# One-hot gate tiles laid out in pairs of tokens, with columns 4 bytes apart in place of 8

## The chip, the core and the metric

The kernel runs on one core of a Trainium2 chip. The metric is device time in microseconds of one execution; lower is better. The engines named below are TensorE (PE in the profile, its weight loads PEld), VectorE (DVE), ScalarE (ACT), GpSimd (POOL), and the DMA queues, which SyncE issues (SP).

## What is computed

One decoder layer for 256 tokens of width 1024: a combined input projection, a convolution module and a sparse attention, an output projection, a memory cross-attention, and at the end a mixer of experts (`peer`) with a final RMSNorm. The change lies in the expert mixer. Each token n picks 8 x 16 = 128 experts out of 16384; an expert's number is a pair (i1, i2) of numbers below 128, and each pick has a gate:

```
def chunk(args):
    xc, ec, gc = args
    u = u_emb[ec]
    a = jax.nn.gelu(jnp.einsum('nd,nkd->nk', xc, u))
    return jnp.einsum('nk,nkd->nd', gc * a, v_emb[ec])
```

The kernel does not gather rows of `u_emb` and `v_emb`. It computes the activations of all 16384 experts for all tokens, multiplies them by a gate that is zero where an expert was not picked, and multiplies the product by all of `v_emb`.

## The kernel before

**Stages.** All activations lie transposed, with features on the 128 partitions and the 256 tokens along the free dimension. Projections in fp32 run as three matmuls in fp32r, on a high and a low part of each operand: `wchunk` (lines 143 to 145) loads 128x1024 weights into a `raw` tile, ScalarE rounds each half to `hi` (line 137), and VectorE (in some stages GpSimd) subtracts to get `lo` (line 138). `proj` and `mm3` (lines 147 to 154) then run 8 x 3 matmuls of 256 columns for a chunk. The tags `hi` and `lo` have six buffers of half a chunk each, `raw` has four.

The expert mixer has three stages.

1. Lines 994 to 999: the first J = 36 chunks of u (128 experts each), whose gelu goes to `slA`. In the last turns the picks of each token are transposed: `i1T`, `i2T` and `gTh`, `gTl` (the gate's high and low fp16 part) are [128 picks, 256 tokens] in fp16.
2. Lines 1024 to 1038, the fused stage: the other 92 chunks of u, and between them 64 turns of `gates4`, one for each four tokens. The loop runs a turn as soon as `ng` falls behind `(i - J) * T // (KEYS - 3 - J)`, so there are 64 turns over 89 chunks.
3. Lines 1073 to 1096: the 128 chunks of v, multiplied by the gated activations and summed in the four PSUM tiles Y.

**A turn of gates4** (lines 1004 to 1022). For four tokens it builds four one-hot tiles on VectorE with 512 fp16 elements per partition. A partition is a pick; the elements are 128 values i times 4 tokens j. `o1` is 1 where i equals the pick's i1 (line 1011), `o2` the same for i2 (line 1012), `oh` and `ol` are `o2` times the high and the low part of the gate (lines 1013, 1014). TensorE multiplies, for each token j, `o1[:, :, j]` (the weights, which are loaded anew for each of the two matmuls) by `oh[:, :, j]` and then by `ol[:, :, j]` (the moving operand; lines 1016, 1017) and sums the two in the PSUM tile `pw`: the 128x128 matrix of this token's gates by (i1, i2). The profile writes the four one-hot tiles all as `o`. VectorE multiplies `pw` into the activations that are there already (line 1021), and ScalarE copies the rest into `slB` (line 1022), for later chunks to be multiplied into (line 1034).

In the old layout the four tokens of one value i lie side by side, so from one value i to the next within one token's tile there are 4 elements, or 8 bytes. The lines that say it:

```
o1, o2, oh, ol = [tmp.tile([P, P, 4], F16, ...) for t in range(4)]
V.tensor_tensor(o1, iota4, over_i(i1T), op=ALU.is_equal)
PE.matmul(pw[:, j], o1[:, :, j], oh[:, :, j], start=True, stop=False)
PE.matmul(pw[:, j], o1[:, :, j], ol[:, :, j], start=False, stop=True)
```

**Order of the work.** TensorE's instructions run in the order in which they are written (`manual_schedule`, line 97); the scheduler orders those of the other engines. `o1`, `oh` and `ol` have two buffers each, `o2` one; `pw` has two PSUM banks (tag `w`), the `pu` tiles of the chunks two others (tag `s`).

One row used below lies elsewhere: line 482 (`ph`) multiplies weights by every 16th f32 column of a tile `KV`, so that its moving columns lie 64 bytes apart. Lines 560 and 883 are matmuls on dense bf16 tiles, lines 442, 591, 596 and 843 on plain f32.

Of the kernel before, what the change touches and what calls it, by code (L numbers as in the profile page):

```python
# [12 lines left out]
F16 = mybir.dt.float16  # L13
# [3 lines left out]
ALU = mybir.AluOpType  # L17
# [3 lines left out]
P = 128  # L21
# [71 lines left out]
def build(tc, A, out, dbg=None):  # L93
    nc = tc.nc
    V, S, G, PE = nc.vector, nc.scalar, nc.gpsimd, nc.tensor
# [13 lines left out]
    def C(name):  # L109
        a, b = CC[name]  # L110
        return con1[:, a:b] if b <= NCON1 else con2[:, a - NCON1:b - NCON1]
# [50 lines left out]
    i1T, i2T, gTh, gTl = [tk.tile([P, T], F16, name=n) for n in ("i1T", "i2T", "gTh", "gTl")]  # L162
# [314 lines left out]
    for i in range(2):  # L477
# [3 lines left out]
        for jj in range(16):  # L481
            PE.matmul(phv, w1[i][:, jj], KV[i][:, :, 2 * jj:2 * jj + 16 * (NC_CMP - 1) + 1:16],
                      start=(jj == 0), stop=(jj == 15))
# [398 lines left out]
    for nh, c in ((0, 0), (1, 0), (1, 1), (0, 1)):  # L882
        PE.matmul(Y[nh][c], zero[:, 0:P], zero, start=True, stop=False, skip_group_check=True)
        for k in range(4):
            PE.matmul(Y[nh][c][:, k * P:(k + 1) * P], h2T[:, 4 * c + k, nh * P:(nh + 1) * P], C("ident"),
                      start=False, stop=False, skip_group_check=True)
# [9 lines left out]
    for hf in range(2):  # L896
# [36 lines left out]
        for side in range(2):  # L933
# [12 lines left out]
            oh = tp.tile([P, 16, P], F16, name=f"ohx{hf}{side}", tag="ohx")  # L946
# [36 lines left out]
    e1 = outer.enter_context(tc.tile_pool(name="e1", bufs=1, side="left", **RW))  # L983
    slA = e1.tile([P, J, T], F32, name="slA")
    tmp = outer.enter_context(tc.tile_pool(name="tmp", bufs=2, side="left", **RW))
    iota4 = tmp.tile([P, P, 4], F16, name="iota4", bufs=1)
    V.tensor_copy(iota4, C("iota").unsqueeze(2).to_broadcast([P, P, 4]))

    def u_chunk(i):
        ps = pp.tile([P, 512], F32, name=f"pu{i}", tag="w" if i < J - 8 and i % 4 > 1 else "s", bufs=2)[:, 0:T]  # L990
# [12 lines left out]

    def gates4(n0, done):
        pw = pp.tile([P, 512], F32, name=f"pw{n0}", tag="w", bufs=2).rearrange("p (n i) -> p n i", n=4)
        o1, o2, oh, ol = [tmp.tile([P, P, 4], F16, name=f"o{t}{n0}", tag=f"o{t}", bufs=1 if t == 1 else 2) for t in range(4)]

        def over_i(t):
            return t[:, n0:n0 + 4].unsqueeze(1).to_broadcast([P, P, 4])

        V.tensor_tensor(o1, iota4, over_i(i1T), op=ALU.is_equal)
        V.tensor_tensor(o2, iota4, over_i(i2T), op=ALU.is_equal)
        V.tensor_tensor(oh, o2, over_i(gTh), op=ALU.mult)  # L1013
        V.tensor_tensor(ol, o2, over_i(gTl), op=ALU.mult)
        for j in range(4):
            PE.matmul(pw[:, j], o1[:, :, j], oh[:, :, j], start=True, stop=False)  # L1016
            PE.matmul(pw[:, j], o1[:, :, j], ol[:, :, j], start=False, stop=True)  # L1017
        for sl_, x0, x1 in ((slA, 0, J), (slB, J, done)):
            if x1 > x0:
                va = sl_[:, 0:x1 - x0, n0:n0 + 4].rearrange("p i n -> p n i")  # L1020
                V.scalar_tensor_tensor(va, pw[:, :, x0:x1], 1.0 / GSC, va, op0=ALU.mult, op1=ALU.mult)  # L1021
        S.activation(slB[:, done - J:, n0:n0 + 4].rearrange("p i n -> p n i"), pw[:, :, done:], AF.Copy, scale=1.0 / GSC)  # L1022

    i, ng = J, 0
    while i < KEYS or ng < T:
        if i < KEYS:
            ps = u_chunk(i)
            if ng:
                tt = tmp.tile([P, T], F32, name=f"ua{i}", tag="ua", bufs=3)
                S.activation(tt[:, 0:ng], ps[:, 0:ng], AF.Gelu_apprx_tanh)  # L1030
            if ng < T:
                S.activation(slB[:, i - J, ng:], ps[:, ng:], AF.Gelu_apprx_tanh)
            if ng:
                V.tensor_mul(slB[:, i - J, 0:ng], slB[:, i - J, 0:ng], tt[:, 0:ng])
            i += 1
        while ng < min(T, (i - J) * T // (KEYS - 3 - J)):
            gates4(ng, i)
            ng += 4
# [35 lines left out]
    for i in range(KEYS):  # L1074
        a = slA[:, i] if i < J else slB[:, i - J]
# [94 lines left out]
```

## Time and profile before

| | |
|---|---|
| median of 3 runs | 1144.11 us (1143.82 to 1146.87) |
| the profiled execution, its own time | 1143.92 us |
| its span in the trace | 1142.1 us |
| TensorE busy | 1095.2 us, 96% |
| TensorE weight loads busy | 1005.4 us, 88% |
| VectorE busy | 884.2 us, 77% |
| ScalarE busy | 591.8 us, 52% |
| GpSimd busy | 111.2 us, 10% |
| mean granted clock of TensorE | 0.984 of full speed |

The span is the time from the first to the last record of the trace; the time of the execution is 1.8 us longer. Busy time counts stretches in which at least one record of the engine is open. A TensorE record includes the passage through the array, so successive records overlap, and the cost of a matmul in a full stream is the distance from its start to the next start, not its length. The records of VectorE overlap a little as well.

### The profile page before, as it was taken

To read this page: it belongs to the slowest core of one execution; us is meant where nothing else is said; L and a number is where in the kernel's file an instruction comes from. 1 tells how busy PE (TensorE), PEld (TensorE's weight loads), DVE (VectorE), ACT (ScalarE), POOL (GpSimd) and SP (SyncE) were. 2 spreads that over 40 slices of the span, in tenths; PEclk is the share of its full clock that TensorE was granted. 3 is DMA by queue.
4 is the path that set the end of the run, shared out by engine and by line. 5 is a ranking of instruction groups with operands and counts; after the bars stand their busy time and mean duration, and the time that the engine had idled before them with its cause. 6 is when DMAs were issued, how large, how long until landed. Compare 5 with 4: busy or idle time off the path is not lost.

```text
span 1142.1 us, 20622 instructions
## 1 busy us (share of the span) xinstructions
PE 1095.2 (96%) x7361; PEld 1005.4 (88%) x7362; DVE 884.2 (77%) x2229; ACT 591.8 (52%) x1354; POOL 111.2 (10%) x86
## 2 busy tenths in 40 slices
PE   8889999999999489999999999999999999999997
PEld 7878778999999489999999999999888888888885
DVE  7998847888889994778888889996666666666665
ACT  5731456665455155555555554445555555555554
POOL 0000000000068389000000000000000000000000
PEclk9899999999999889999999999999999999999999
DMA  8542224625434235544444454446555566565662
GB/s 277 194 127 94 74 99 152 197 90 185 154 124 149 93 114 200 167 156 141 150 147 160 137 161 137 151 144 203 191 196 193 194 192 195 192 196 191 196 192 86
DMA packets 51688, 182.47 MB, mean 160 GB/s; under 512 B 5761, under 2 KB 6529, under 8 KB 51457
## 3 DMA queue, kind: packets, MB, share of 16 engines
q1 hardware_dynamic: 51296, 180.62, 48.2%
q8 instruction: 58, 0.95, 0.3%
q10 hardware_dynamic: 288, 0.52, 0.1%
q14 instruction: 46, 0.37, 0.1%
HBM read 179.81 MB, written 1.05 MB: 158 GB/s over the span
## 4 chain that ended last, share of the span: by engine, by line
PE 87%; DVE 4%; issue 3%; POOL 2%; DMA 1%; ACT 1%; SPq 0%; POOLq 0%; ACTq 0%; DVEq 0%
PE Y L1070 30%; PE pu L150 10%; PE pu L149 10%; PE pu L148 10%; PE pw L1016 3%; PE pw L1017 3%; PE pmk L442 3%; POOL lo L138 2%; PE pmv L458 2%; PE ppq L148 1%; PE ppq L149 1%; PE ppq L150 1%; DVE lo L138 1%; PE pmw L149 1%; PE pmw L148 1%
## 5 line engine op out<-in xcount | busy, mean ns | idle before, releaser
L137 ACT ACTIVATE hi<-raw 128x512 fp32r<-128x512 f32 x632 | 380.6, 624 | 198.7 <-PE pu L149 78.0
L138 DVE TENSOR_TENSOR lo<-raw,hi 128x512 fp32r<-128x512 f32 (+1 forms) x560 | 371.1, 685 | 32.8 <-ACT hi L137 26.4
L148 PE MATMUL pu<-hn_h,hi 128*128 128x256 f32 x1024 | 296.9, 290 | 18.3 <-ACT hi L137 18.3
L150 PE MATMUL pu<-hn_h,lo 128*128 128x256 f32 x1024 | 291.6, 285 | 2.5 <-POOL lo L138 2.5
L149 PE MATMUL pu<-hn_l,hi 128*128 128x256 f32 x1024 | 290.8, 284 | 0.0
L148 PEld LDWEIGHTS pu<-hn_h,hi 128*128 128x128 f32 x1024 | 198.0, 193 | 18.7 <-ACT hi L137 18.5
L150 PEld LDWEIGHTS pu<-hn_h,lo 128*128 128x128 f32 x1024 | 196.7, 192 | 4.6 <-POOL lo L138 4.5
L149 PEld LDWEIGHTS pu<-hn_l,hi 128*128 128x128 f32 x1024 | 197.2, 193 | 0.0
L1070 PE MATMUL Y<-hi,ah 128*128 128x512 f32 x512 | 158.2, 389 | 0.0
L1070 PE MATMUL Y<-lo,ah 128*128 128x512 f32 x512 | 158.1, 389 | 0.0
L1070 PE MATMUL Y<-hi,al 128*128 128x512 f32 x512 | 158.1, 389 | 0.0
L1070 PEld LDWEIGHTS Y<-lo,ah 128*128 128x128 f32 x512 | 96.1, 188 | 20.0
L1070 PEld LDWEIGHTS Y<-hi,al 128*128 128x128 f32 x512 | 96.1, 188 | 19.8
L1070 PEld LDWEIGHTS Y<-hi,ah 128*128 128x128 f32 x512 | 96.1, 188 | 19.9
L158 DVE TENSOR_TENSOR al<-slB,ah 128x256 fp32r<-128x256 f32 x92 | 39.1, 425 | 89.9 <-PE Y L1070 89.9
L138 POOL TENSOR_TENSOR lo<-raw,hi 128x512 fp32r<-128x512 f32 x72 | 103.7, 1473 | 36.6 <-ACT hi L137 36.3
L157 ACT ACTIVATE ah<-slB 128x256 fp32r<-128x256 f32 x92 | 38.5, 418 | 115.7 <-PE Y L1070 115.7
L1022 ACT ACTIVATE slB<-pw 128x364 f32<-128x364 f32 (+31 forms) x64 | 33.3, 521 | 67.3 <-DVE slB L1021 50.1
L1017 PE MATMUL pw<-o,o 128*128 128x128 f16 x256 | 64.2, 297 | 0.0
L1016 PE MATMUL pw<-o,o 128*128 128x128 f16 x256 | 63.6, 294 | 0.0
L273 DVE SCALAR_TENSOR_TENSOR yc<-u,par,yc 128x256 f32<-128x256 f32 x120 | 55.9, 477 | 0.3
L1013 DVE TENSOR_TENSOR o<-o,gTh 128x512 f16<-128x512 f16 x64 | 28.5, 445 | 30.9 <-PE pw L1016 30.5
(387 smaller groups left out, 1754.1 us busy)
## 6 DMA issues: line engine op xcount, KB each, us to landing
raw<-u SPq DMA_DIRECT2D x128, 512.0 KB, 3.3
raw<-v SPq DMA_DIRECT2D x128, 512.0 KB, 4.3
raw<-peer_w_q SPq DMA_DIRECT2D x16, 512.0 KB, 3.3
raw<-w_in_t SPq DMA_DIRECT2D x15, 512.0 KB, 6.0
raw<-w_mem_k SPq DMA_DIRECT2D x8, 512.0 KB, 3.4
raw<-w_mem_v SPq DMA_DIRECT2D x8, 512.0 KB, 3.4
raw<-w_out SPq DMA_DIRECT2D x8, 512.0 KB, 3.9
raw<-w_mem_q SPq DMA_DIRECT2D x8, 512.0 KB, 3.3
```

The costliest lines, as they stand in the source:

```text
L137: S.activation(hi, r, AF.Copy)
L138: (engs or (V, V))[q].tensor_sub(lo, r, hi.bitcast(F32))
L148: PE.matmul(ps, w[0], xh, start=start, stop=False)
L149: PE.matmul(ps, w[0], xl, start=False, stop=False)
L150: PE.matmul(ps, w[1], xh, start=False, stop=stop)
L157: S.activation(dst[0], src, AF.Copy)
L158: V.tensor_sub(dst[1], src, dst[0].bitcast(F32))
L273: V.scalar_tensor_tensor(yc[:, i], u[:, i, j:j + T], w, yc[:, i], op0=ALU.mult, op1=ALU.add)
L442: PE.matmul(ps, wr[:, k * P:(k + 1) * P], mg[:, k], start=(k == 0), stop=(k == KC - 1))
L1016: PE.matmul(pw[:, j], o1[:, :, j], oh[:, :, j], start=True, stop=False)
L1017: PE.matmul(pw[:, j], o1[:, :, j], ol[:, :, j], start=False, stop=True)
L1070: PE.matmul(Y[nh][c], lhs[:, sl], wc[c][t], start=False, stop=i == KEYS - 1 and lhs is a[1], skip_group_check=True)
```

## The change

The one-hot tiles become [128, 2, 128, 2]: two blocks of two tokens. Within a block the two tokens of one value i lie side by side, so that within one token's tile the step from one value i to the next is 2 elements, or 4 bytes. The tile with the numbers 0 to 127 is repeated twice in place of four times and read by both blocks. Nothing else is changed: the number of instructions, their order on each engine, the sizes of the matmuls and of the four VectorE operations, the buffers and the values are the same. The only instruction with another count of elements is the copy that fills the tile of numbers (line 987), which has 256 elements per partition in place of 512. The lines behind line 1008 have higher numbers in the changed kernel (the one-hot operations one more, the matmuls and what follows two more).

```diff
-    iota4 = tmp.tile([P, P, 4], F16, name="iota4", bufs=1)
-    V.tensor_copy(iota4, C("iota").unsqueeze(2).to_broadcast([P, P, 4]))
+    iota2 = tmp.tile([P, P, 2], F16, name="iota2", bufs=1)
+    V.tensor_copy(iota2, C("iota").unsqueeze(2).to_broadcast([P, P, 2]))
...
-        o1, o2, oh, ol = [tmp.tile([P, P, 4], F16, name=f"o{t}{n0}", tag=f"o{t}", bufs=1 if t == 1 else 2) for t in range(4)]
+        o1, o2, oh, ol = [tmp.tile([P, 2, P, 2], F16, name=f"o{t}{n0}", tag=f"o{t}", bufs=1 if t == 1 else 2) for t in range(4)]

         def over_i(t):
-            return t[:, n0:n0 + 4].unsqueeze(1).to_broadcast([P, P, 4])
-
-        V.tensor_tensor(o1, iota4, over_i(i1T), op=ALU.is_equal)
-        V.tensor_tensor(o2, iota4, over_i(i2T), op=ALU.is_equal)
+            return t[:, n0:n0 + 4].rearrange("p (a b) -> p a b", b=2).unsqueeze(2).to_broadcast([P, 2, P, 2])
+
+        i4 = iota2.unsqueeze(1).to_broadcast([P, 2, P, 2])
+        V.tensor_tensor(o1, i4, over_i(i1T), op=ALU.is_equal)
+        V.tensor_tensor(o2, i4, over_i(i2T), op=ALU.is_equal)
         V.tensor_tensor(oh, o2, over_i(gTh), op=ALU.mult)
         V.tensor_tensor(ol, o2, over_i(gTl), op=ALU.mult)
         for j in range(4):
-            PE.matmul(pw[:, j], o1[:, :, j], oh[:, :, j], start=True, stop=False)
-            PE.matmul(pw[:, j], o1[:, :, j], ol[:, :, j], start=False, stop=True)
+            q, r = j // 2, j % 2
+            PE.matmul(pw[:, j], o1[:, q, :, r], oh[:, q, :, r], start=True, stop=False)
+            PE.matmul(pw[:, j], o1[:, q, :, r], ol[:, q, :, r], start=False, stop=True)
```

## Rows read from the trace of the kernel before

**Rows 1.** The matmuls into pw: number, shortest, median, longest ns, first and last start.

```profile
L1016 PE MATMUL pw<-o,o x256: 285/296/301, 463.6 to 774.3; 128*128 128x128 f16 x128
L1017 PE MATMUL pw<-o,o x256: 293/297/301, 463.7 to 774.4; 128*128 128x128 f16 x128
```

**Rows 2.** Stretch, length, busy PE, PEld, DVE, ACT, POOL; granted clock, DMA share, GB/s.

```profile
463.00:778.50 315.50, 315.50 (x2640) 312.00 (x2639) 270.69 (x642) 164.47 (x419) 0.00 (x0) 1.00 0.46 149
...
623.00:703.00 80.00, 80.00 (x671) 79.12 (x670) 70.00 (x163) 41.12 (x108) 0.00 (x0) 1.00 0.46 150
703.00:778.50 75.50, 75.50 (x633) 74.68 (x632) 70.30 (x153) 36.68 (x101) 0.00 (x0) 1.00 0.45 150
778.50:1142.10 363.60, 355.92 (x1601) 295.78 (x1599) 227.60 (x413) 192.05 (x395) 2.77 (x1) 0.99 0.57 185
```

**Rows 3.** Timeline of one turn, matmuls and loads together: start us, length us, instruction.

```profile
602.33 0.29 PE L1016 MATMUL pw<-o,o 128*128 128x128 f16 x1
...
602.44 0.12 PEld L1016 LDWEIGHTS <-o 128*128 128x128 f16 x1
602.56 0.30 PE L1016 MATMUL pw<-o,o 128*128 128x128 f16 x1
...
603.15 0.29 PE L1017 MATMUL pw<-o,o 128*128 128x128 f16 x1
...
603.40 0.28 PE L149 MATMUL pu<-hn_l,hi 128*128 128x256 f32 x1
...
603.52 0.28 PE L150 MATMUL pu<-hn_h,lo 128*128 128x256 f32 x1
```

**Rows 4.** Groups of matmuls by shape: number, busy us, mean ns, idle time.

```profile
L149 PE MATMUL pu<-hn_l,hi 128*128 128x256 f32 x1024 | 290.8, 284 | 0.0
L1070 PE MATMUL Y<-hi,ah 128*128 128x512 f32 x512 | 158.2, 389 | 0.0
...
L843 PE MATMUL psq<-skp,pqt 128*128 128x128 f32 x64 | 9.2, 274 | 0.0
...
L482 PE MATMUL ph<-KV,w 128*128 128x45 f32 x64 | 8.9, 272 | 0.0
...
L560 PE MATMUL pss<-causb,identb 128*128 128x128 bf16 x32 | 4.6, 224 | 0.0
...
L883 PE MATMUL Y<-zero 128*128 128x512 bf16 x3 | 1.1, 378 | 0.9 <-ACT sco L846 0.9
```

**Rows 5.** The same view for weight loads.

```profile
L149 PEld LDWEIGHTS pu<-hn_l,hi 128*128 128x128 f32 x1024 | 197.2, 193 | 0.0
...
L1016 PEld LDWEIGHTS <-o 128*128 128x128 f16 x256 | 29.6, 116 | 3.1
...
L596 PEld LDWEIGHTS po<-PT,vn 128*64 128x64 f32 x32 | 3.0, 136 | 1.3 <-issue 1.3
...
L560 PEld LDWEIGHTS <-identb 128*128 128x128 bf16 x32 | 1.8, 97 | 4.0 <-issue 2.9
...
L591 PEld LDWEIGHTS po<-pcT,vcp 128*128 128x128 f32 x8 | 1.5, 191 | 0.2
```

**Rows 6.** TensorE's timeline around two dense bf16 matmuls.

```profile
104.09 0.28 PE L560 MATMUL pss<-causb,identb 128*128 128x128 bf16 x2
104.21 0.43 PE L442 MATMUL pmk<-mg,raw 128*128 128x256 f32 x1
```

**Rows 7.** VectorE's groups, 463 to 778 us.

```profile
L138 DVE TENSOR_TENSOR lo<-raw,hi 128x512 fp32r<-128x512 f32 x177 | 120.8, 690 | 14.2 <-ACT hi L137 12.8
...
L1012 DVE TENSOR_TENSOR o<-iota,i2T 128x512 f16<-128x512 f16 x61 | 25.6, 420 | 0.0
```

**Rows 8.** Waits in 703 to 778 us: total us, times, longest.

```profile
ACT hi L137 <- PE pu L149: 11.6, 21, 0.8
...
DVE o L1013 <- PE pw L1016: 5.1, 6, 1.0
...
DVE lo L138 <- ACT hi L137: 0.8, 1, 0.8
```

## The prediction

> **What bounds the kernel now.** I read five views in this order: the busy times by stretch, to see which engine has no slack where the edit sits; the instructions of one turn of that stage, for the distance between starts; the groups of TensorE's matmuls and weight loads by shape, for what a column costs at other spacings; VectorE's groups, for the one-hot work; the waits, for who would be late next.
>
> The one-hot tiles are used only in the fused stage, from the first pw matmul at 463.6 us to the last at 774.4 us [rows 1]. Over 463 to 778.5 us TensorE is busy for 315.50 of 315.50 us, at a granted clock of 1.00, which is the 2.4 GHz level; VectorE is busy for 270.69, ScalarE for 164.47, and the DMA share is 0.46 [rows 2]. TensorE is the bound there without a gap, so time taken from its instructions is time off the end. Its work adds up: 89 chunks of u with 24 matmuls each, one every 0.12 us, are 256 us, and 512 pw matmuls, one every 0.117 us, are 60 us; together 316.
>
> The spacing of the pw matmuls is read in one turn: the first starts at 602.33 and the eighth at 603.15 us, seven steps of 0.117 us; from the first to the second pu matmul behind them (603.40) are 1.07 us, and with 0.12 for one pu the eight cost 0.95 [rows 3]. A pw matmul has 128 columns; a pu matmul, with 256, takes 0.12. So a column of the one-hot tile costs 0.91 ns and one of pu at most 0.47.
>
> **Whether the spacing of the columns is the reason.** A record's length is a fixed part plus its columns. Dense bf16, columns 2 bytes apart: 512 columns 378 ns, 128 columns 224 ns, so 0.40 ns a column and 173 ns fixed. fp32r, whose columns lie 4 bytes apart: 512 columns 389 ns, 256 columns 284 ns, so 0.41 a column [rows 4]. A pw matmul takes a median 296 or 297 ns for 128 columns [rows 1]; less 173 that is 0.96 a column, 2.4 times as much, at 8 bytes apart. One more row has wide steps: the ph matmuls (line 482) read columns 64 bytes apart and take 272 ns for 45 columns, where plain f32 takes 274 ns for 128 columns side by side [rows 4]. So the reading of the moving operand pays for distance, and at 4 bytes fp32r pays nothing. The tile moved here is fp16 at 4 bytes; no row has that, and this is the step I take on trust from the fp32r rows.
>
> The weights could be the bound instead, as they are read with the same spacing. Their load takes 116 ns here and 97 dense [rows 5]. Plain f32 loads take 136 ns for 64 columns and 191 for 128, so 0.86 a column and some 81 ns that are latency [rows 5]; less 81, the loads of this stage stream for 35 ns, the dense ones for 16. The pu loads, 193 ns long, sit in a rhythm of 0.12 us [rows 3, 5], so a record longer than the spacing does not set it. Against this stands that in rows 3 each pw matmul starts just when the load ahead of it ends; that becomes a rival.
>
> **The change, part by part.**
>
> *The 512 pw matmuls.* No engine's instruction order changes. Bounds for the new spacing: nothing gained (0.117, the rows as they are), or one column per 0.41 ns, 0.053 us. The nearest row lies near the lower end: two 128-column bf16 matmuls, each with a weight load of its own, start at 104.09 and the next matmul at 104.21, 0.060 each [rows 6]. I take 0.060, since it holds the handover between load and matmul. Gain: 512 x 0.057 = 29 us; by the bounds 0 to 33.
>
> A rule that speaks against this: the Trainium skill, page "Advanced Engine Details and Errata", section "Memory Cachelines", says that SBUF is read in lines of 16 bytes, and that two hits on a line are enough to hide the access. Columns 8 bytes apart have two per line, so by it the old layout is already at full speed and the gain is nothing, 1144 us; the trace disagrees, with 0.96 against 0.40 ns a column.
>
> *The 256 one-hot operations on VectorE* (four per turn, 64 turns) keep their 512 fp16 elements, but the innermost run of the index and gate operands shrinks from four elements to two. Those on i2 take 420 ns; 512 f32 elements take 690 [rows 7]. So they run at a packed pace, and the bounds are 0 and 256 x 0.27 = 69 us of VectorE's time. I take 0, because a run of two still fills one pair; the other end is a rival. The copy of iota has half the elements, once, ahead of the stage: nothing.
>
> *What is late next.* VectorE. With 29 us gone the stage has 287 us against VectorE's 271. Early there is room: up to 623 us VectorE is busy for what the later rows leave of its 270.69, 130 us, and TensorE keeps 160 - 15 = 145. In 623 to 703 it is 70.00 busy against 73, and in 703 to 778.5 it is 70.30 against 75.5 - 7.0 = 68.5 (a share of 29 us by length): 1.8 us short [rows 2]. The lead covers it at first: ScalarE still waits 11.6 us in that stretch, 21 times, for TensorE to free hi buffers, and VectorE 5.1 us for TensorE to free one-hot buffers, so both run ahead of TensorE to the very end [rows 8]. The hi and lo tags hold six halves, three chunks; two chunks ahead are some 6 us of TensorE work. I charge 2 us, between 0 and 5 (the 1.8 us, and three more of VectorE's in-order waits on TensorE and ScalarE, the longest of which are 1.0 and 0.8 [rows 8]). ScalarE, at 164 of 287, and the DMA, whose 150 GB/s would be 165 where the next stage moves 185 [rows 2], stay free. After the stage VectorE falls to 227.60 of 363.60 [rows 2], so nothing is handed on.
>
> *Sum.* 29 - 2 = 27 us off. The profiled execution took 1143.92 us (span 1142.1 and 1.8 around it); the median of three runs is 1144.11, so the sum may stand on either. Forecast: 1117 us. With the bounds of this case (spacing 0.053 to 0.070, VectorE 0 to 5 us): 33 to 19 off, 1111 to 1125.
>
> **The rivals.**
>
> *A, the load sets the rhythm.* In rows 3 load and matmul alternate end to start. If a load must be through before the next matmul can go, the spacing falls only to the dense load's 97 ns, or partway. Gain 512 x 0.020 = 10 us at 97 ns, and half of the main gain, 15, halfway: 1129 to 1134 us. For it: that alternation over a train of eight, where rows 6 have two. Against: loads of 97 ns lie in the 0.060 rhythm of rows 6, and loads of 193 ns in the 0.12 of pu. The Trainium skill, page "TensorE: Matmul & The Clock Gate", section "Back-to-back issue gap", gives about 81 ns per matmul for a sustained stream of loads and 128-column matmuls; by it the gain is 512 x 0.036 = 18 us, 1126 us, and no train that long with dense columns stands in this trace.
>
> *B, the spacing was not the cause, or 4 bytes of fp16 cost as 8 do.* Then nothing moves: VectorE has slack and the order is the same: 1144 us. For it: 2-byte elements at 4 bytes are in no row. Against: the 0.41 of fp32r at the same distance, and that the step of 64 bytes costs still more. The rule on lines of 16 bytes, above, would end here too.
>
> *C, VectorE's one-hot operations lose their packed pace.* Each would need a step of the access pattern per pair. At 690 ns VectorE's work becomes 271 + 69 = 340 us, more than the 315.5 of the stage; at 95 to 100% busy the stage takes 340 to 358, 24 to 42 us more: 1168 to 1186, some 1175 us. It decides from the point at which VectorE's work passes 315.5, 45 us more, or 0.175 us for each operation; below 287, 0.06 us for each, it costs almost nothing, between them it eats the gain. For it: no row has a run of two. Against: four already broke the run every two pairs, at 420 ns.
>
> **How the numbers follow.** Main case 0.74, A 0.11, B 0.09, C 0.06. The predicted time is the main case's, 1117 us. Its own range is 1111 to 1125. A range of 1111 to 1129 takes in the upper half of A's gains and leaves out B, C and the weak end of A, some 0.19. A run of this kernel can be told from no change at about 0.3%, 3.4 us. Main and A lie beyond that: faster 0.85. B: same 0.09. C: slower 0.06.
>
> **What would show it.** Right: pw matmuls 0.06 us apart and some 225 ns long, the eight of a turn in about 0.5 us in place of 0.95; one-hot operations still at 420 ns; VectorE above 90% busy after 620 us, ScalarE's waits for hi buffers shorter; the last pw matmul some 27 us earlier, and the next stage as long as before. Wrong: pw spacing still 0.117 (B) or close to the length of its load (A); one-hot operations near 690 ns and TensorE waiting for lo (C); gaps on TensorE late in the stage that sum to over 5 us, by which VectorE would have become the bound sooner than I charge.

## The result, and the profile after

The changed kernel takes 1117.37 us (median of 4 runs, 1116.28 to 1118.19), the kernel before on the same chip 1145.49 us (4 runs). The ratio is 0.976, with a 95% interval of 0.9745 to 0.9774. The forecast was 1117.0 us, 1111 to 1129.

The matmuls into pw are line 1018 (oh) and line 1019 (ol) now. Their records in the changed kernel, with shortest, median and longest length in ns and the first and last start in us, to be held against [rows 1]:

```profile
L1018 PE MATMUL pw<-o,o x256: 218/218/231, 464.1 to 747.8; 128*128 128x128 f16 x128
L1019 PE MATMUL pw<-o,o x256: 218/218/220, 464.2 to 747.9; 128*128 128x128 f16 x128
```

A record has fallen from 296 to 218 ns, near the 224 of a dense bf16 matmul of the same size [rows 4]. From the first to the last pw are 283.8 us where there were 310.8: 27.0 us less. One turn in the timeline (start us, length us):

```profile
577.70 0.28 PE L149 MATMUL pu<-hn_l,hi 128*128 128x256 f32 x1
...
577.82 0.28 PE L150 MATMUL pu<-hn_h,lo 128*128 128x256 f32 x1
577.94 0.10 PEld L1018 LDWEIGHTS <-o 128*128 128x128 f16 x1
577.94 0.23 PE L1018 MATMUL pw<-o,o 128*128 128x128 f16 x1
577.95 0.10 PEld L1019 LDWEIGHTS <-o 128*128 128x128 f16 x1
578.01 0.22 PE L1019 MATMUL pw<-o,o 128*128 128x128 f16 x1
...
578.35 0.22 PE L1019 MATMUL pw<-o,o 128*128 128x128 f16 x1
...
578.38 0.36 PE L148 MATMUL pu<-hn_h,hi 128*128 128x256 f32 x1
...
578.58 0.28 PE L149 MATMUL pu<-hn_l,hi 128*128 128x256 f32 x1
```

Read as [rows 3] were: from the first pw to the second pu are 0.64 us, less 0.12 for one pu is 0.52, where it was 0.95. 64 turns x 0.43 us = 27.5 us. The steps within the turn are 0.41 us for seven, 0.058 each. The remaining 0.06 us of a turn lie at its ends: the second pw comes 0.07 behind the first, and the first pu, which seems to start at once, is followed only 0.20 us later.

The stretches of the changed kernel (columns as in [rows 2]; the cuts are scaled, roughly, to the shorter stage):

```profile
463.00:751.50 288.50, 288.50 (x2641) 285.75 (x2641) 267.75 (x639) 162.47 (x418) 0.00 (x0) 1.00 0.51 163
463.00:608.00 145.00, 145.00 (x1332) 143.58 (x1331) 127.64 (x323) 86.26 (x209) 0.00 (x0) 1.00 0.50 162
608.00:681.00 73.00, 73.00 (x667) 72.36 (x665) 70.24 (x165) 40.39 (x108) 0.00 (x0) 1.00 0.52 167
681.00:751.50 70.50, 70.50 (x649) 69.81 (x648) 69.87 (x153) 35.81 (x103) 0.00 (x0) 1.00 0.50 160
751.50:1115.60 364.10, 356.35 (x1605) 296.11 (x1603) 228.47 (x416) 193.08 (x399) 2.77 (x1) 1.00 0.58 186
```

TensorE is still busy without a gap, 288.50 of 288.50 us, and the next stage has kept its length (364.10 against 363.60). VectorE is busy for 69.87 of the last 70.5 us. Its one-hot operations keep their pace, 417 ns where [rows 7] have 420, by its groups of 463 to 751 us:

```profile
L1013 DVE TENSOR_TENSOR o<-iota,i2T 128x512 f16<-128x512 f16 x61 | 25.4, 417 | 0.0
```

The waits of 680 to 751 us (total us, times, longest) show a shorter lead:

```profile
ACT hi L137 <- PE pu L149: 7.0, 11, 0.8
...
DVE o L1014 <- PE pw L1018: 0.4, 1, 0.4
```

ScalarE waits for hi buffers 11 times in place of 21 [rows 8], and VectorE practically no more for one-hot buffers: 0.4 us in place of 5.1. The weight loads (columns as in [rows 5]) are as short as the dense ones there:

```profile
L1019 PEld LDWEIGHTS <-o 128*128 128x128 f16 x256 | 25.0, 98 | 0.0
L1018 PEld LDWEIGHTS <-o 128*128 128x128 f16 x256 | 23.3, 96 | 2.8
```

### The profile page after: what moved, and what is told of

It reads as the page before. It is cut to its first block, busy times and chain, and to the rows that moved or that the text cites. A ratio compares the mean times of both kernels' runs of the same rounds, so it can differ in the third digit from the quotient of the medians.

```text
span 1115.6 us, 20623 instructions
## 1 busy us (share of the span) xinstructions
PE 1069.5 (96%) x7362; PEld 980.5 (88%) x7362; DVE 882.1 (79%) x2229; ACT 590.1 (53%) x1354; POOL 111.2 (10%) x86
## 4 chain that ended last, share of the span: by engine, by line
PE 87%; DVE 5%; issue 4%; POOL 2%; ACT 2%; DMA 0%; SPq 0%; POOLq 0%; ACTq 0%; DVEq 0%
PE Y L1072 31%; PE pu L148 10%; PE pu L150 10%; PE pu L149 10%; PE pmk L442 3%; POOL lo L138 2%; PE pmv L458 2%; PE pw L1018 1%; PE ppq L148 1%; PE ppq L149 1%; PE ppq L150 1%; PE pw L1019 1%; DVE lo L138 1%; PE pmw L149 1%; PE pmw L148 1%
## 5 line engine op out<-in xcount | busy, mean ns | idle before, releaser
L158 DVE TENSOR_TENSOR al<-slA,ah 128x256 fp32r<-128x256 f32 x36 | 15.3, 425 | 33.6 <-PE Y L1072 33.6
L1012 DVE TENSOR_TENSOR o<-iota,i1T 128x512 f16<-128x512 f16 x64 | 28.6, 448 | 12.7 <-ACT i1T L976 12.7
L157 ACT ACTIVATE ah<-slA 128x256 fp32r<-128x256 f32 x36 | 15.0, 418 | 44.1 <-PE Y L1072 43.0
```

The lines of the kernel that those rows point to most:

```text
L157: S.activation(dst[0], src, AF.Copy)
L158: V.tensor_sub(dst[1], src, dst[0].bitcast(F32))
L1012: V.tensor_tensor(o1, i4, over_i(i1T), op=ALU.is_equal)
```

## The experiments

The ratios below are to the kernel before, run beside each experiment. Two theories stood against each other. By the first, the old spacing of the pw matmuls came from the reading of the moving operand, whose cost per column grows with the distance of the columns. By the second (rival A), it came from the weight load, which read tiles with the same spacing. A third question was how near VectorE is to being the bound, and a fourth whether the cost goes by distance or by lines of memory.

**Moving tiles alone.** o1, the weights, goes back to fours; oh and ol stay in pairs.

```diff
-            PE.matmul(pw[:, j], o1[:, q, :, r], oh[:, q, :, r], start=True, stop=False)
-            PE.matmul(pw[:, j], o1[:, q, :, r], ol[:, q, :, r], start=False, stop=True)
+            PE.matmul(pw[:, j], o1[:, :, j], oh[:, q, :, r], start=True, stop=False)
+            PE.matmul(pw[:, j], o1[:, :, j], ol[:, q, :, r], start=False, stop=True)
```

> Weights (o1) stay at 8 bytes between columns, the moving tiles (oh, ol) go to 4. If the reading of the moving operand set the old rhythm: pw matmuls 0.057 to 0.060 us apart and 218 to 226 ns long, their loads still 116 ns, time 1115 to 1120 us like the changed kernel. If the weight load set it (rival A): spacing 0.117 us as before the change, 1144 us.

Measured: 1120.73 us, ratio 0.9794 (0.9773 to 0.9815). The records of the first of each two pw matmuls, and the group of the loads:

```profile
L1023 PE MATMUL pw<-o,o x256: 218/222/250, 464.4 to 750.0; 128*128 128x128 f16 x128
```

```profile
L1024 PEld LDWEIGHTS <-o 128*128 128x128 f16 x256 | 30.3, 118 | 0.0
L1023 PEld LDWEIGHTS <-o 128*128 128x128 f16 x256 | 27.7, 113 | 2.8
```

The loads are about as long as in the old kernel (113 to 118 ns against 116 in [rows 5]) and yet nearly all of the gain is there. One turn, from its first pw to the second pu behind it:

```profile
601.82 0.25 PE L1023 MATMUL pw<-o,o 128*128 128x128 f16 x1
...
602.50 0.28 PE L149 MATMUL pu<-hn_l,hi 128*128 128x256 f32 x1
```

Less one pu that is 0.56 us in place of 0.52, 64 x 0.04 = 2.6 us by this turn; from the first to the last pw are 285.6 us in place of 283.8, 1.8 us more. The profiled execution took 1119.49 us, 2.1 more than that of the changed kernel, so the turns account for most of the difference.

**Weights alone.** The reverse: o1 in pairs, oh and ol in fours.

```diff
+            PE.matmul(pw[:, j], o1[:, q, :, r], oh[:, :, j], start=True, stop=False)
+            PE.matmul(pw[:, j], o1[:, q, :, r], ol[:, :, j], start=False, stop=True)
```

> The other half alone: weights (o1) at 4 bytes, moving tiles (oh, ol) back at 8. Moving operand as the cause: spacing 0.117 us, length 296 ns, loads 96 ns, 1142 to 1147 us. Weight load as the cause: spacing 0.057 us, 1117 us. If both must be close for the gain, this and the run with the other half both give 1144.

Measured: 1145.71 us, ratio 1.0006 (0.9996 to 1.0015). The same two views:

```profile
L1023 PE MATMUL pw<-o,o x256: 278/296/300, 466.4 to 776.2; 128*128 128x128 f16 x128
```

```profile
L1024 PEld LDWEIGHTS <-o 128*128 128x128 f16 x256 | 28.8, 112 | 0.1
```

The length is the old 296 ns, the spacing the old 0.117 us, and nothing is gained. One detail was not as expected: the loads took 112 ns and not 96, although their tile lies in pairs. Only the moving reads are wide here, so the load's record lengthens with those too; which of them does it is taken up with the run at 16 bytes.

**Dense tiles.** Each token's tile contiguous (and the tile of numbers with it), 2 bytes between columns; the operands from i1T, i2T, gTh and gTl then repeat one element along the innermost run.

```diff
-        o1, o2, oh, ol = [tmp.tile([P, 2, P, 2], F16, ...
+        o1, o2, oh, ol = [tmp.tile([P, 4, P], F16, ...
...
-            return t[:, n0:n0 + 4].rearrange("p (a b) -> p a b", b=2).unsqueeze(2).to_broadcast([P, 2, P, 2])
+            return t[:, n0:n0 + 4].unsqueeze(2).to_broadcast([P, 4, P])
```

> Each token's tile dense (2 bytes between columns), so that VectorE's index and gate operands repeat one element along the innermost run. TensorE: spacing 0.055 to 0.057 us, nothing more to gain below 4 bytes. VectorE: if the run of the repeated operand decides its pace (rival C's mechanism), the one-hot operations go from 417 to about 690 ns, VectorE's work in the stage from 268 to 337 us, and the stage to 337 to 355 in place of 288: 1166 to 1184 us, TensorE waiting for lo. If the pace holds: 1117 us.

Measured: 1154.7 us, ratio 1.0086 (1.0063 to 1.011). VectorE's group and the stretch of the stage:

```profile
L1013 DVE TENSOR_TENSOR o<-iota,i2T 128x512 f16<-128x512 f16 x61 | 41.1, 674 | 0.0
```

```profile
463.00:790.00 327.00, 297.20 (x2644) 287.55 (x2643) 326.64 (x640) 161.72 (x420) 0.00 (x0) 1.00 0.43 143
```

TensorE's records are no better than the 218 ns at 4 bytes:

```profile
L1017 PE MATMUL pw<-o,o x256: 216/219/230, 464.1 to 785.9; 128*128 128x128 f16 x128
```

VectorE's operations slow down from 417 to 674 ns. VectorE is then busy for 326.64 of 327.00 us and TensorE idle for 30. So rival C's mechanism exists, at a repeated single element, and it turns the gain into a loss; a run of two escapes it. The price was set too high: I expected 337 to 355 us for the stage. The 247 one-hot operations of the stretch grew by 0.257 us each, 63 us, where 256 at 690 ns would be 70; VectorE's other operations took some 4 us less in all (`lo`, line 138, 674 ns in place of 685); and VectorE filled its time to the last, where I had allowed for less.

**The distance.** oh alone at 16 and at 12 bytes between columns, o1 and ol at 4. The values written are the same; the tile has gaps.

```diff
+        oh = oh8[:, :, 0:4].rearrange("p i (a b) -> p a i b", b=2)
```

where `oh8` is [P, P, 8]; in the other run it is [P, P, 6].

> The changed kernel with oh alone at 16 bytes between columns (ol and o1 stay at 4). 256 of the 512 pw matmuls read wide. If the cost grows with the distance: spacing 0.23 us behind those, 256 x 0.18 = 45 us, 1160 to 1165 us. If a wide column costs a fixed amount, the same as at 8 bytes: 0.117 us, 15 us more, 1132 us. If the wide half hides beside the narrow half: 1117 us.

> As the run with oh at 16 bytes, but at 12. There the wide matmul held TensorE for 0.215 us, 1.68 ns a column, where 8 bytes took 0.117 and 4 bytes 0.057. If the cost grows by 4 bytes at a time: 0.16 us, 1.26 ns a column, time some 25 us over the changed kernel, 1143 us. If it goes by lines of 16 bytes (a column in 12 bytes mostly opens a new line, as at 16): 0.2 us or more, 1155 to 1160 us. If by lines of 8 bytes: likewise 0.2 us.

Measured: 1160.29 us at 16 bytes (ratio 1.0135, 1.0114 to 1.0156) and 1146.96 us at 12 (one run). TensorE's timeline at 16 bytes, where line 1019 reads oh and line 1020 ol:

```profile
602.88 0.39 PE L1019 MATMUL pw<-o,o 128*128 128x128 f16 x1
603.10 0.24 PE L1020 MATMUL pw<-o,o 128*128 128x128 f16 x1
603.17 0.39 PE L1019 MATMUL pw<-o,o 128*128 128x128 f16 x1
```

and at 12 bytes:

```profile
604.55 0.33 PE L1019 MATMUL pw<-o,o 128*128 128x128 f16 x1
604.70 0.24 PE L1020 MATMUL pw<-o,o 128*128 128x128 f16 x1
604.78 0.33 PE L1019 MATMUL pw<-o,o 128*128 128x128 f16 x1
```

The wide matmul holds TensorE for 0.22 us at 16 bytes and 0.15 at 12, where 8 took 0.117 and 4 take 0.058. At 0.053 us for 128 columns at full pace [rows 4] these are about 4, 3, 2 and 1 times as much: from 4 to 16 bytes the cost goes up in step with the distance. TensorE had no gap in either run. The two times stand 43 and 30 us above the changed kernel (1117.37, and 1117.04 when it ran beside the run at 12), where 45 and 25 were expected. The narrow matmul behind a wide one also takes a little longer, 0.07 to 0.08 us in place of 0.058.

This does not settle the fourth question. If every new line of 16 bytes cost the same and nothing else counted, the four costs would come out alike: of four columns in a row 1, 2, 3 and 4 open a new line at 4, 8, 12 and 16 bytes. The expectation for 12 bytes took nearly every column for a new line, but it is three in four. The two theories part beyond 16 bytes, and no fp16 run goes there. The one row that does is ph, f32 at 64 bytes [rows 4]: with the fixed 173 ns of the prediction, (272 - 173) / 45 = 2.2 ns a column against (274 - 173) / 128 = 0.79 for f32 side by side, 2.8 times as much at 16 times the distance. So the growth does not go on at that rate for f32; where it ends for fp16 is open.

The loads of the run at 16 bytes speak to the detail left above:

```profile
L1019 PEld LDWEIGHTS <-o 128*128 128x128 f16 x256 | 28.8, 112 | 23.2
L1020 PEld LDWEIGHTS <-o 128*128 128x128 f16 x256 | 25.0, 98 | 0.0
```

In the timeline the load for a matmul opens when the matmul ahead of it starts, so line 1020's loads open beside a wide matmul and line 1019's beside a narrow one, just behind a wide one. It is the latter that are long, so running beside a wide read is not what lengthens them; why they are longer is open.

**More work for VectorE.** The changed kernel with the operation that makes ol issued twice.

```diff
         V.tensor_tensor(ol, o2, over_i(gTl), op=ALU.mult)
+        V.tensor_tensor(ol, o2, over_i(gTl), op=ALU.mult)
```

> The changed kernel with the fourth one-hot operation of each turn issued twice (64 more on VectorE, some 0.33 us of its time each, 21 us). If VectorE is just at its limit late in the stage of the changed kernel (69.87 us busy of 70.5 in 681 to 751.5), the late part lengthens: 140 us of work in 608 to 751.5 become 151 against TensorE's 143.5, less the lead of a few us: 3 to 8 us more, 1120 to 1125 us, with gaps on TensorE. If VectorE still has room (its busy share being inflated by records that overlap or stretch): 1117 us. If its in-order waits make every added us count: 21 us, 1138 us.

**The base.** The changed kernel once more, unedited, beside the three runs with an added operation, with turns two by two and with 12 bytes.

> The changed kernel itself, on the chip of this call, as the base for the other three: 1115 to 1120 us.

Measured: the base 1117.04 us (ratio 0.9758, 0.9745 to 0.9771), the kernel with the extra operation 1124.66 us (0.9821, 0.9806 to 0.9836), 7.6 us more. Its stretches:

```profile
463.00:608.00 145.00, 145.00 (x1328) 143.62 (x1327) 135.24 (x351) 86.39 (x208) 0.00 (x0) 1.00 0.50 165
608.00:681.00 73.00, 73.00 (x670) 72.31 (x669) 72.76 (x176) 37.58 (x105) 0.00 (x0) 1.00 0.48 158
681.00:758.00 77.00, 73.81 (x659) 71.50 (x658) 76.76 (x174) 33.94 (x103) 0.00 (x0) 1.00 0.45 149
```

VectorE is full from 608 us on, and TensorE, without a gap until 681, is idle for 3.2 us of the next 77. Most of that idle time is put down to ScalarE (463 to 745 us: a group of matmuls with its idle time, and a wait):

```profile
L148 PE MATMUL pu<-hn_h,hi 128*128 128x256 f32 x685 | 199.4, 291 | 2.3 <-ACT slB L1035 2.2
ACT slB L1025 <- DVE slB L1024: 76.3, 46, 3.4
```

Line 1035 is ScalarE's reading of the `pu` tile, and ScalarE itself waits for VectorE, 76.3 us in that stretch against 52.0 in the base. So VectorE's lateness reaches TensorE through ScalarE. The changed kernel stands near the point where VectorE becomes the bound: of some 21 us added (estimated before the run; VectorE's busy time in the whole span grew by 22.7), 13 or 14 were still covered. Some 2 us of the 7.6 came before the stage (the first pw starts at 465.7 us against 463.7 in the base); why stays open.

**Turns two by two.** An attempt at a faster version: two turns back to back, so that TensorE changes between pw and pu 32 times in place of 64.

```diff
             gates4(ng, i)
-            ng += 4
+            gates4(ng + 4, i)
+            ng += 8
```

> The changed kernel with two turns of four tokens back to back. Each change from pw to pu and back costs TensorE some 0.065 us over the plain rhythm (a turn takes 0.52 us, eight matmuls at 0.057 are 0.46), and there are 32 changes in place of 64: 2 us less, 1115 us. Against it: the tiles for the second turn of a pair are needed at once, all double buffers of o and both pw banks are in use in the same moment, and VectorE is 99 per cent busy late in the stage, so TensorE may wait for one-hot tiles or lo: 1118 to 1125 us.

Measured: 1115.82 us, ratio 0.975 (0.9737 to 0.9763), beside 0.9758 (0.9745 to 0.9771) for the base. The median is 1.2 us lower, where 2 were expected, but the intervals overlap: no difference is shown. In the stretch of the stage TensorE is as good as never idle:

```profile
463.00:749.50 286.50, 286.33 (x2638) 284.75 (x2638) 264.99 (x640) 165.75 (x418) 0.00 (x0) 1.00 0.51 163
```

## Why the prediction was right, point by point

*The bound.* TensorE had no gap in the stage before and has none after, so every us taken from its instructions came off the end. 27.5 us by the turns, 27.0 us by the first and last pw, 27 to 28 us by the medians (against 1144.11 and 1145.49): the same within the spread of the runs.

*The cause.* The step taken on trust was that fp16 columns at 4 bytes read as fast as fp32r columns at 4 bytes. The records of 218 ns show it, and dense tiles are no faster (219). That it is the moving operand and not the load is shown by the two halves: the moving half alone gives 1120.73 us, the weight half alone 1145.71. Rival A, and B with it, are out. The rule of 16-byte lines in the Trainium skill, page "Advanced Engine Details and Errata", section "Memory Cachelines", by which two columns to a line, at 8 bytes, would have been free, does not hold for this reading: 8 bytes cost about twice, 12 three times and 16 four times what 4 do. That lines play no part is not shown by this.

*The spacing.* Forecast 0.060 us from two dense matmuls in a row, measured 0.058 within a turn of eight. The Trainium skill, page "TensorE: Matmul & The Clock Gate", section "Back-to-back issue gap", gives about 81 ns for such a stream; over a train of eight this trace shows 58 ns, and so does the train of sixteen in the run with turns two by two.

*Two terms of the sum were off by a little, in opposite directions.* The term 512 x 0.057 = 29 us left out that the ends of a turn do not shrink with it: per turn 0.06 us remain over the plain rhythm, where the old turn had 0.01. By turns it is 27.5. The 2 us charged to VectorE did not come: with 69.87 of 70.5 us busy it stayed just within its time. That the sum still came to 27 is luck in this point: some 1.7 us promised too much and 2 us charged too much cancel. The run with an added operation shows that the margin was not wide: 21 us of work more, some 8% of what VectorE does in the stage, cost 7.6 us.

*The slower rival.* VectorE kept its packed pace at a run of two (417 ns). The dense run shows that the rival was a real danger one step further: at 674 ns the time is 1154.7, below the 1168 to 1186 that I gave it, since VectorE's work in the stage grew by 59 us (326.64 against 267.75), not 69, from 268 us and not 271, and all its idle time was used up.

## What to carry to other kernels

Where a matmul's moving operand is taken out of an interleaved tile, look at the bytes from one column to the next: in these runs, fp16 columns at 4 to 16 bytes, each 4 bytes of distance beyond the first cost about one more pass of the operand, while weights at 8 bytes cost next to nothing. At 2 bytes nothing more was gained, and beyond 16 this growth is not shown. Interleave so that 2-byte columns come to lie 4 bytes apart, and check that the engine that writes the tile still has a run of two, because the dense layout cost it its pace here and gained TensorE nothing. Before counting on such a gain, add up what the next engine does in the same stage; here VectorE had room for this change and not much more.

## What the runs showed that was not expected

The weights' spacing is not quite free: at 8 bytes a turn of eight takes 0.56 us in place of 0.52, and a load 113 to 118 ns in place of 96. The load's record also lengthens to 112 ns when only the moving tiles are wide, and in the run at 16 bytes it does so behind a wide matmul, not beside one. And VectorE pays for gaps in what it writes: the operation that makes oh takes 641 ns at 16 bytes, in a kernel where the one that makes ol, in pairs, takes 452:

```profile
L1015 DVE TENSOR_TENSOR o<-o,gTh 128x512 f16<-128x512 f16 x64 | 41.0, 641 | 40.9 <-PE pw L1019 40.9
L1016 DVE TENSOR_TENSOR o<-o,gTl 128x512 f16<-128x512 f16 x64 | 28.9, 452 | 0.0
```
